# A one-core hybrid attention layer: attention by tiles of rows with the output projection between them, one chunk of 512 columns for two, and a query stack by turns

## The chip, the cores and the metric

The kernel runs on one core of one Trainium2 chip. The metric is device time of one execution in microseconds (us), the median of several runs. The core's engines are PE (matrix products), DVE (vector), ACT (scalar functions and copies), POOL (general purpose) and SP (which issues the transfers). Each runs its own instructions in order, and they wait for each other by semaphores. PEld is PE's loading of stationary operands, which runs beside its products.

## What is computed

The reference is one decoder layer over 512 rows of 1024 features, in float32. A combined projection feeds two groups of eight heads of 64:

```python
h = rms_norm(x, norm_gain)
proj = jnp.einsum('bsd,dc->bsc', h, w_in)          # 3420 columns
# group A: compressed blocks, selected blocks, sliding window; sigmoid gates
o_nsa = g[..., 0:1] * o_cmp + g[..., 1:2] * o_sel + g[..., 2:3] * o_win
o_nsa = o_nsa.reshape(B, S, NSA_WIDTH) * jax.nn.silu(z_n)
# group B: a relu indexer picks 128 keys per query, which are attended
o_dsa = dsa_branch(qd, kd, heads(v_d, Gd), qi_r, ki_r, wi)
o_dsa = o_dsa.reshape(B, S, DSA_WIDTH) * jax.nn.silu(z_d)
mixed = jnp.concatenate([o_nsa, o_dsa], axis=-1)
return x + jnp.einsum('bsc,cd->bsd', mixed, w_out)
```

With 512 rows all eight selected blocks and the whole window are taken, so both are causal attention with different keys and values. The indexer's choice is a mask found by sixteen rounds of "eight largest, strike them out".

## The kernel before, in words

**Precision.** Nearly every product is made of parts: a float32 operand is split in a high part (a cast on ACT, `nc.scalar.copy`) and a low part (a subtraction on DVE or POOL, `split`, L338 and L339), and PE multiplies high by high, high by low and low by high.

**Chunks.** The columns of `w_in` are cut into chunks (`CHUNKS`), each projected for four tiles of 128 rows (`proj`, L372) or transposed (`projT`, L382). `queue_chunk` issues a chunk's loads (256 KB each) and splits; the halves live in a ring of `WBUFS` = 4 slots of 1024 columns, so that a chunk of 256 columns takes two slots and one of 512 columns four. I holds the indexer, C and B the keys and values of group A, Q1 and Q2 its queries (heads of g = 0 and 1), E the keys and values of group B, D its queries, Z0 to Z3 the gates z. `chunk` runs a projection and after each tile its evacuation (norm sums on ACT, rotation on DVE and POOL).

**Attention.** The work is cut into units: `n` i g b is group A, row tile i, head group g, branch b (1 selected, 2 window, 0 compressed), `d` i g 0 is group B. For each (i, g) `qstack` transposes the queries (L577, into one of two S banks of PSUM) and stacks them for the score products: high parts in rows 0 to 63 and again in 64 to 127 (L582, L584, ACT), low parts in a second block (L583, DVE) whose lower rows are zero. `kstack` puts the keys' high parts in rows 0 to 63 (L561) and the low parts in 64 to 127 (L562). The score products (L934, L935) then need two passes. `softmax_of` adds the mask and finds the maximum (L916, DVE), takes exponentials (L918, ACT) and scales (L930, POOL). `transposed` turns the probabilities (L970) and splits them (L971, L972); `times_values` multiplies by the values (L981); `combine` adds the parts (L1008 ACT, L1009 DVE); `mix` multiplies by z and splits the result (L1126 to L1128).

**Output.** `out_half(i, half)` is half of the output projection of row tile i: 24 products over four blocks of `mixed` (L1147), in the two `mm` banks that the projections also use (the last tile's third part in an S bank). Half 0 needs group A's result of that tile, half 1 group B's.

**Order.** `weave` writes the program: it takes attention steps and fills in other work, by credits, until a named unit has ended. Before the change: group A g = 0, tiles 3 to 0, with Q2, E and D as fill; group A g = 1, tiles 3 to 0, with the z chunks and the loads of `wout`; group B, tiles 3 to 0, with `out_half`. Then `set_order` orders all instructions of each engine anew: a list scheduler that runs forward and backward eight times with a cost model, keeps the order with the earliest modelled end and writes it down as dependencies. Its model adds `AGAIN` to ACT instructions that read PSUM, by what went before.

Of the kernel before, what the change touches and what calls it, by code (L numbers as in the profile page):

```python
# [29 lines left out]
    ("E", [(2328, 2584)]),  # L30
# [4 lines left out]
    ("Q2", [(256, 512)]),  # L35
# [27 lines left out]
ARENA = 2824 + 1536 + 256 + 512  # L63
ARENA_R = 5376
# [33 lines left out]
AGAIN = 45, 112, 0  # L98

SPARE = 200  # L100

# [3 lines left out]
def set_order(tc):  # L105
# [40 lines left out]
    def reads_bank(i, e):  # L146

        if e != "Activation":
            return None
        return any("PSUM" in str(getattr(ap.bass_ap.tensor, "space", "")) for w, ap in aps(i) if not w)  # L150
# [62 lines left out]
    bank = [reads_bank(i, e) for i, e in zip(insts, eng)]  # L213
    sums = [len(list(i.outs)) > 1 for i in insts]
# [4 lines left out]
    def turns(due, back=False):  # L219
# [12 lines left out]
        last = [2]  # L232
        there = [0.0] * LANES
        for _ in range(count):
# [4 lines left out]
            k = min((k for k in l if ready[k] <= now), key=lambda k: due[k] + PORT * late * port[k])  # L239
# [11 lines left out]
            if bank[k] is not None:  # L251
                if bank[k]:
                    more = AGAIN[last[0]]
                last[0] = 2 if sums[k] else int(bank[k])
# [37 lines left out]
def tile_hybrid_layer(ctx, tc, xT, x, ng, win, gains, peT, w1, b1, w2, wout, cst, out):  # L292
# [199 lines left out]
    gns = carve([6, 2 * HD], F32)  # L492
    nc.sync.dma_start(gns, gains.rearrange("(o a) b -> o a b", o=1).partition_broadcast(128))
    tabs = carve([2, 2, NT, HD], F32)
    tturn = [0]

    def tables(j, name):
        gn = gns[:, j, None, :]
        c, s = (tabs[:, tturn[0] % 2, x] for x in range(2))
        tturn[0] += 1  # L500
# [51 lines left out]

    def kstack(dst, R, h0, nh, back=False):

        p = ps("T", "kT_ps")
        for t in range(NT):
            c = (NT - 1 - t if back else t) * 128
            nc.tensor.transpose(p[:nh * HD, c:c + 128], R[:, t, h0:h0 + nh, :], ident)
# [5 lines left out]
    qbufs = []  # L564
    for i in range(2):
        qb = carve([2, 4, 128], F32R)
        nc.gpsimd.memset(qb[64:128, 1].bitcast(F32), 0.0)
        qbufs.append(qb)
    qcount = [0]

    def qstack(R, t):
# [16 lines left out]
    ridx = b8.tile([128, NT, 5, HD], F32, tag="ridx", name="ridx")  # L588
    rest = work.tile([128, NT, 28], F32, tag="rest", name="rest", bufs=1)
    for t in (0, 1, 2, 3):  # L590
        p = Ips[t]
        rope(ridx[:, t, 4:5], p[:, :64], 1, cosd[:, t:t + 1, :], sind[:, t:t + 1, :], add=nc.vector)
# [10 lines left out]
    nc.gpsimd.tensor_tensor(ridx[:, :, 4], ridx[:, :, 4], rb.to_broadcast([128, NT, HD]), op=ALU.mult)  # L603
# [10 lines left out]
    kdi = b8.tile([128, 3, S], F32R, tag="kdi", name="kdi")  # L614
# [3 lines left out]
    scores = b8.tile([128, 1152], F32, tag="scores", name="scores")  # L618
    masks = b8.tile([128, 1152], BF16, tag="masks", name="masks")

    def indexer():
        kstack([kdi[:, 2, :]], ridx, 4, 1)
# [3 lines left out]
        for i in (3, 2, 1):  # L626
# [3 lines left out]
            s0 = 64 * i * (i + 1) - 128  # L630
            sc = scores[:, s0:s0 + n]
            for h in range(4):
                p = ps("S", f"idx{i}{h}")
                nc.tensor.matmul(p[:, :n], q[:, 0, h, :], kdi[:, 2, :n], start=True, stop=False)
                nc.tensor.matmul(p[:, :n], q[:, 1, h, :], kdi[:, 2, :n], start=False, stop=True)
# [12 lines left out]
            mbias[i] = masks[:, s0:s0 + n]  # L648
# [14 lines left out]
    kn = [b8.tile([128, 2 * S + 32], F32R, tag=f"kn{g}", name=f"kn{g}") for g in range(2)]  # L663
# [19 lines left out]
    def chunk_C(kv):  # L683
        p = ps("mm", f"C_{kv}")
# [93 lines left out]
    def hidden3():  # L778
        kp = ps("S", "kc_ps")[:64, :64]
        nc.tensor.transpose(kp, FSs["kr"], ident[:64, :64])  # L780
        for g in range(2):
            dst = kn[g][:, K_CMP:K_CMP + 32]
            src_ = kp[:, 32 * g:32 * g + 32]
            nc.scalar.copy(dst[0:64], src_)
            nc.vector.tensor_tensor(dst[64:128], src_, dst[0:64].bitcast(F32), op=ALU.subtract)
        yield 0.1
# [47 lines left out]
    def kb_stack():  # L834
        for b in range(2):
            kstack([k[:, 0:S] if b else k[:, K_SEL:] for k in kn], ST["kb_raw"][b], 0, 2, back=bool(b))
# [4 lines left out]
    def e_first():  # L841
        ST["kd_raw"] = work.tile([128, NT, 2, HD], F32, tag="m2", name="kd_raw", bufs=2)
# [7 lines left out]
    def kd_stack():  # L850
        kstack([kdi[:, 0, :], kdi[:, 1, :]], ST["kd_raw"], 0, 2)
        yield 0.4
# [4 lines left out]
    def queries(name, key, j, gs, nxt, after=()):  # L857

        def first():
# [4 lines left out]
            for g in gs:  # L864
                Rs[key, g] = b8.tile([128, NT, 4, HD], F32, tag=f"R_{key}{g}", name=f"R_{key}{g}")
                ST["ss" + key, g] = sums(f"{key}{g}")

        def evac(p, t):
            for x, g in enumerate(gs):
                heads_of(p[:, 256 * x:256 * x + 256], ST["ss" + key, g], t, Rs[key, g], 4, ST["tab" + key])  # L870

        def done():
            for g in gs:
                norm_of(rs[key, g], ST["ss" + key, g], 4)

# [138 lines left out]
    def units_of(kind, i, g, done):  # L1014
# [20 lines left out]
        if kind == "d":  # L1035
            u.v = [pair(vd[:, j, g]) for j in range(i + 1)]
            u.S = lambda: softmax_steps(kdi[:, g, :max(n, 256)], [(u, slice(0, n), mbias[i])])
# [10 lines left out]
        if i == 0:  # L1048
            us.S = lambda: softmax_steps(k[:, w0:K_SEL + n], [sel(n + 32), win_, cmp(n)])
        else:  # L1050
            uw.S = lambda: softmax_steps(k[:, w0:S], [win_])
            if i < 3:
                us.S = lambda: softmax_steps(k[:, K_CMP:K_SEL + n], [sel(32), cmp(0)])
            else:
                us.S = lambda: softmax_steps(k[:, K_SEL:], [sel(0)])
                uc.S = lambda: compressed_steps(uc, k[:, K_CMP:K_SEL], cmask[:, i, :])
# [33 lines left out]
    def attention(units):  # L1090
# [4 lines left out]
        for k, u in enumerate(units):  # L1095
            ahead.setdefault(max(k - (2 if u.kind == "n" else 1), 0), []).append(u)
# [119 lines left out]
    weave(att, "n010", [  # L1216
# [107 lines left out]
```

## Time and profile before

| what | value |
| --- | --- |
| median of 3 runs | 320.56 us (320.38 to 320.7) |
| the profiled execution | 320.34 us |
| its span, first to last instruction | 318.6 us |
| busy in the span: PE, DVE, ACT, POOL | 312.5, 256.1, 248.1, 243.0 us |
| PE products | 1789 |
| TensorE clock granted | full speed in all 40 slices |

Rows are in us unless marked ns. PE is busy 98% of the span, but the ends of its products are modelled and overlap the next one's start, so short gaps do not show as idle time. Whether PE works or waits is read from the distance of the starts of neighbouring products, against the distance in a stretch without waits.

### The profile page before, as it was taken

How to read it: one execution, taken by the hardware profiler on the slowest of the kernel's cores; microseconds unless marked ns; L12 is line 12 of the kernel's file. 1: busy time of each engine (PE TensorE's matmuls, PEld its weight loads, DVE VectorE, ACT ScalarE, POOL GpSimd, SP SyncE). 2: the span in 40 equal slices, each digit the busy share in tenths (PEclk: the TensorE clock that was granted, in tenths of full speed). 3: DMA queues.
4: the chain of work that ended last, by engine and by line, in shares of the span. 5: the costliest groups of instructions: out<-in, count | busy, mean ns of one | idle time of the engine just before them, and what ended most of it. 6: DMA issues, size and time to landing. Idle time of an engine off the chain costs nothing.

```text
span 318.6 us, 6139 instructions
## 1 busy us (share of the span) xinstructions
PE 312.5 (98%) x1789; PEld 267.7 (84%) x1789; DVE 256.1 (80%) x773; ACT 248.1 (78%) x813; POOL 243.0 (76%) x418
## 2 busy tenths in 40 slices
PE   8999999999999999999999999999999999999995
PEld 5997888999989998888887888788877778888885
DVE  4978532999999999999999999999997887825301
ACT  6962855999889999899998988889988999943200
POOL 3179897988998999886699999995859987873200
PEclk9999999999999999999999999999999999999999
DMA  7990553445230133000031053021220533403011
GB/s 256 417 352 33 139 160 115 150 116 181 70 99 2 37 99 100 2 1 0 3 87 47 2 165 88 16 82 48 69 66 2 163 102 100 149 19 102 31 66 66
DMA packets 14945, 30.28 MB, mean 95 GB/s; under 512 B 1792, under 2 KB 2176, under 8 KB 14912
## 3 DMA queue, kind: packets, MB, share of 16 engines
q1 hardware_dynamic: 14912, 29.90, 30.0%
q8 instruction: 14, 0.23, 0.3%
q14 instruction: 19, 0.16, 0.2%
HBM read 27.79 MB, written 2.10 MB: 94 GB/s over the span
## 4 chain that ended last, share of the span: by engine, by line
PE 62%; DVE 21%; ACT 9%; issue 3%; DMA 2%; POOL 1%; SPq 1%; DVEq 0%; POOLq 0%
PE out L1147 13%; PE D L372 7%; PE B L372 7%; PE on L981 5%; PE T_n L970 4%; PE E L372 4%; PE z L382 4%; DVE scores L647 3%; DVE m L646 3%; PE od L981 3%; DMA xw<-in_xT_dram 2%; DVE P_d L916 2%; PE s_n L934 2%; DVE ptl L972 2%; PE s_n L935 2%
## 5 line engine op out<-in xcount | busy, mean ns | idle before, releaser
L918 ACT ACTIVATE P_n<-P_n,arena 128x512 f32<-128x512 f32 (+3 forms) x64 | 35.9, 563 | 4.2 <-DVE arena L916 3.7
L930 POOL TENSOR_SCALAR P_n<-P_n,arena 128x512 f32<-128x512 f32 (+3 forms) x64 | 33.2, 538 | 1.5
L916 DVE CUSTOM_DVE_ANT_0 P_n<-s_n,arena 128x512 f32<-128x512 f32 (+3 forms) x64 | 34.0, 542 | 0.3
L972 DVE TENSOR_TENSOR ptl<-T_n,pth 128x512 fp32r<-128x512 f32 x40 | 27.2, 683 | 0.6 <-ACT pth L971 0.2
L382 PE MATMUL z<-hThi,whi_Z 128*128 128x512 f32 x64 | 27.0, 422 | 0.1
L646 DVE MAX8 m<-scores 128x8 f32<-128x512 f32 (+2 forms) x48 | 26.4, 550 | 0.2
L647 DVE MATCH_REPLACE8 scores<-m,scores 128x512 f32<-128x512 f32 (+2 forms) x48 | 26.0, 541 | 0.1
L382 PE MATMUL z<-hThi,wlo_Z 128*128 128x512 f32 x64 | 25.4, 396 | 0.0
L382 PE MATMUL z<-hTlo,whi_Z 128*128 128x512 f32 x64 | 25.2, 393 | 0.0
L970 PE MATMUL T_n<-arena,P_n 128*128 128x128 f32 x160 | 24.6, 272 | 0.0
L1147 PE MATMUL out<-wohi,mx 128*128 128x512 f32 (+1 forms) x72 | 23.5, 377 | 0.0
L971 ACT CAST pth<-T_n 128x512 fp32r<-128x512 f32 x40 | 23.1, 581 | 0.4
L970 PEld LDWEIGHTS T_n<-arena,P_n 128*128 128x128 f32 x160 | 19.9, 140 | 3.7
L1147 PE MATMUL out<-whi_wo,mx 128*128 128x512 f32 (+1 forms) x72 | 22.2, 374 | 0.0
L339 POOL TENSOR_TENSOR wlo_Z<-raw_Z,whi_Z 128x512 fp32r<-128x512 f32 x16 | 20.6, 1303 | 1.6 <-ACT whi_Z L338 1.6
L339 POOL TENSOR_TENSOR w1l<-raw_w,w1h 128x512 fp32r<-128x512 f32 x16 | 20.5, 1294 | 1.5 <-ACT w1h L338 1.4
L972 DVE TENSOR_TENSOR ptl<-T_d,pth 128x512 fp32r<-128x512 f32 x20 | 13.8, 689 | 8.5 <-ACT pth L971 8.3
L930 POOL TENSOR_SCALAR P_d<-P_d,arena 128x512 f32<-128x512 f32 (+3 forms) x32 | 16.7, 543 | 4.2 <-DVE arena L920 4.1
L934 PE MATMUL s_n<-kn,arena_r 128*128 128x512 f32 (+4 forms) x56 | 19.8, 353 | 0.1
L981 PE MATMUL on<-pth,arena_r 128*128 128x512 f32 x48 | 19.8, 413 | 0.0
L918 ACT ACTIVATE P_d<-P_d,arena 128x512 f32<-128x512 f32 (+3 forms) x32 | 17.8, 559 | 1.9 <-DVE arena L916 1.8
L981 PE MATMUL on<-ptl,arena_r 128*128 128x512 f32 x48 | 18.9, 395 | 0.0
(277 smaller groups left out, 1193.2 us busy)
## 6 DMA issues: line engine op xcount, KB each, us to landing
raw_w<-in_w_dram SPq DMA_DIRECT2D x16, 256.0 KB, 3.0
raw_Z<-in_win_dram SPq DMA_DIRECT2D x16, 256.0 KB, 2.7
wor<-in_wout_dram SPq DMA_DIRECT2D x16, 256.0 KB, 2.8
raw_Q<-in_win_dram SPq DMA_DIRECT2D x8, 256.0 KB, 2.8
raw_D<-in_win_dram SPq DMA_DIRECT2D x8, 256.0 KB, 2.7
xres<-in_x_dram SPq DMA_DIRECT2D x8, 256.0 KB, 2.8
out_dram<-xres SPq DMA_DIRECT2D x7, 256.0 KB, 2.0
xw<-in_xT_dram SPq DMA_DIRECT2D x2, 860.0 KB, 8.7
```

Of the source, the lines that this page charges most:

```text
L339: engine.tensor_tensor(lo, raw, hi.bitcast(F32), op=ALU.subtract)
L372: nc.tensor.matmul(out_ps, a[:, k, tsl], b, start=(k == 0 and b is hi and a is hT["hi"]), stop=(k == KB - 1 and a is hT["lo"]))
L382: nc.tensor.matmul(out_ps, b[:, csl], a[:, k, :], start=(k == 0 and b is hi and a is hT["hi"]), stop=(k == KB - 1 and b is lo))
L646: nc.vector.max(m8, sc)
L647: nc.vector.match_replace(sc, m8, sc, -3e38)
L916: nc.vector.tensor_tensor_reduce(P[:, h], src_, mask, u.r[:, h:h + 1], 3e38, op0=ALU.add, op1=ALU.min, accum_out=m[:, h:h + 1])
L918: nc.scalar.activation(P[:, h], P[:, h], AF.Exp, bias=m[:, h:h + 1], scale=-1.0, accum_out=l[:, h:h + 1])
L930: nc.gpsimd.tensor_scalar(P[:, hh], P[:, hh], l[:, hh:hh + 1], 1.0 if u.gate is not None else 0.5, op0=ALU.mult, op1=ALU.mult)
L970: nc.tensor.transpose(p[:, h * 128:(h + 1) * 128], u.P[:, h, j * 128:(j + 1) * 128], ident)
L972: nc.vector.tensor_tensor(pl, p, ph.bitcast(F32), op=ALU.subtract)
L981: nc.tensor.matmul(o, u.v[j], pp, start=(u.first and j == 0 and x == 0), stop=(end and x == 1))
L1147: nc.tensor.matmul(p, a, b[:, csl], start=(k == 0 and b is hi and a is mx[0]), stop=(k == 7 and a is mx[1]))
```

## The change

Five things are changed.

- **One chunk for two.** E is gone from `CHUNKS`; its 256 columns follow those of Q2, and `queries` gets hooks for E's own start, evacuation and end.
- **Query and key stacks.** `qstack` writes the high parts of an odd head into rows 64 to 127 and its low parts into rows 0 to 63, those of an even head the other way round; each query is stacked once, high and low in one column, and multiplied by a key block with high parts in both halves and one with low parts in both halves. `kstack` fills both halves of both blocks by a new helper, `key_parts`. The indexer's key is written twice by POOL, so that its transpose has it in both halves.
- **Order of the attention and the output.** After group A g = 0, each tile does its group A g = 1 units and then its two group B units; the halves of the output projection of a tile stand between the units of the next.
- **The scheduler's model.** `AGAIN` is replaced by `TURN`: 125 ns on ACT and 118 ns on DVE, less idle time, where an instruction starts on other rows than the one before it, and a leaning of a quarter of that to instructions on the same rows. Due times are also carried back along the dependencies.
- **Places.** Chunk C's products stand in O banks and not in mm banks; tables, gains, scores and masks are tiles of their own and not parts of one large tile; the query stack's look-ahead is one unit instead of two where the unit before is of group B.

```diff
 CHUNKS = [
     ("I", [(2840, 2908), (1280, 1304), (2584, 2840)]),
-    ("E", [(2328, 2584)]),
     ("D", [(1816, 2328)]),
...
-    ("Q2", [(256, 512)]),
+    ("Q2", [(256, 512), (2328, 2584)]),
...
-AGAIN = 45, 112, 0
+TURN = {"Activation": 125, "DVE": 118}
+
+CHOICE = 0.25
...
+    def rows_of(i, e):
+
+        if e not in TURN:
+            return None
+        first = []
+        for w, ap in sorted(aps(i), key=lambda x: x[0]):
+            row = list(ap.ap)[0][0]
+            if free(ap) > 1:
+                first.append(ap.bass_ap.offset // row if row else 0)
+        return tuple(first) if any(first) else ()
...
+        if not back:
+            due = [d - h for d, h in zip(due, hurry)]
+            for k in reversed(range(count)):
+                for j in before[k]:
+                    due[j] = min(due[j], due[k] - costs[j][0])
...
-            k = min((k for k in l if ready[k] <= now), key=lambda k: due[k] + PORT * late * port[k])
+            k = min((k for k in l if ready[k] <= now), key=lambda k: due[k] + PORT * late * port[k]
+                    + (CHOICE * TURN[e] if e in TURN and rows[k] != last[e] else 0))
...
-                    more = AGAIN[last[0]]
-                last[0] = 2 if sums[k] else int(bank[k])
+            if e in TURN:
+                if rows[k] != last[e]:
+                    more = max(TURN[e] - (start[k] - idle[e]), 0)
+                last[e] = rows[k]
...
+    def key_parts(dst, src_, o):
+
+        hi, lo = dst
+        at, to = slice(64 * o, 64 * o + 64), slice(64 - 64 * o, 128 - 64 * o)
+        nc.scalar.copy(hi[at], src_)
+        nc.vector.tensor_tensor(lo[at], src_, hi[at].bitcast(F32), op=ALU.subtract)
+        nc.scalar.copy(hi[to], src_)
+        nc.scalar.copy(lo[to], lo[at].bitcast(F32))
+
...
         for g in range(nh):
-            src_ = p[g * HD:(g + 1) * HD, :]
-            nc.scalar.copy(dst[g][0:64], src_)
-            nc.vector.tensor_tensor(dst[g][64:128], src_, dst[g][0:64].bitcast(F32), op=ALU.subtract)
...
+            key_parts(dst[g], p[g * HD:(g + 1) * HD, :], g)
...
-        qv = q.rearrange("p s (a b) q -> p s a b q", b=2)
+        qv = q.rearrange("p (a b) q -> p a b q", b=2)
         for o in range(2):
-            src_ = pv[o * 64:(o + 1) * 64]
-            nc.scalar.copy(qv[0:64, 0, :, o, :], src_)
-            nc.vector.tensor_tensor(qv[0:64, 1, :, o, :], src_, qv[0:64, 0, :, o, :].bitcast(F32), op=ALU.subtract)
-            nc.scalar.copy(qv[64:128, 0, :, o, :], src_)
+            hi, lo = slice(o * 64, o * 64 + 64), slice(64 - o * 64, 128 - o * 64)
+            nc.scalar.copy(qv[hi, :, o, :], pv[hi])
+            nc.vector.tensor_tensor(qv[lo, :, o, :], pv[hi], qv[hi, :, o, :].bitcast(F32), op=ALU.subtract)
         return q
...
-        p = ps("mm", f"C_{kv}")
+        p = ps("O", f"C_{kv}")
...
     def scores_of(p, q, h, k):
-        nc.tensor.matmul(p, q[:, 0, h, :], k, start=True, stop=False)
-        nc.tensor.matmul(p, q[:, 1, h, :], k, start=False, stop=True)
+        for x in range(2):
+            nc.tensor.matmul(p, q[:, h, :], k[:, x], start=(x == 0), stop=(x == 1))
...
     units = []
-    for g in range(2):
-        for i in (3, 2, 1, 0):
-            units += units_of("n", i, g, nothing)
     for i in (3, 2, 1, 0):
+        units += units_of("n", i, 0, nothing)
+    for i in (3, 2, 1, 0):
+        units += units_of("n", i, 1, nothing)
         for g in range(2):
-            units += units_of("d", i, g, lambda i=i, g=g: mix(1, i, g))
+            units += units_of("d", i, g, nothing if i == 3 else lambda i=i, g=g: mix(1, i, g))
     att = attention(units)
     weave(att, "n000", [
-        queries("Q2", "q", 0, [1], "E", {0: hidden3(), 1: hidden1(1), 3: hidden2(1)}),
-        call(queue_chunk, "D"),
-        chunk("E", e_evac, lambda: norm_scale([ST["kd_raw"]], ST["ss_kd"]), e_first),
+        queries("Q2", "q", 0, [1], "D", {0: hidden3(), 1: hidden1(1), 3: hidden2(1)},
+                (e_first, lambda p, t: e_evac(p[:, 256:], t), lambda: norm_scale([ST["kd_raw"]], ST["ss_kd"]))),
         queries("D", "d", 3, [0, 1], "Z0"),
         kd_stack(),
     ], RA, X1, LEAD)
-    weave(att, "n010", [
+    weave(att, "d310", [
         zchunk(0, "Z1"),
...
-    for g in range(2):
-        mix(0, 3, g)
-    weave(att, "d310", [out_half(3, 0)], 0.0, X3)
+    for half in range(2):
+        for g in range(2):
+            mix(half, 3, g)
     for i in (2, 1, 0):
+        weave(att, f"n{i}10", [out_half(i + 1, 0)], RA, X3)
         for g in range(2):
             mix(0, i, g)
-        weave(att, f"d{i}10", [out_half(i + 1, 1), out_half(i, 0)], RA, X4)
-    weave((), None, [out_half(0, 1)], 1.0)
+        weave(att, f"d{i}10", [out_half(i + 1, 1)], RA, X4)
+    weave((), None, [out_half(0, 0), out_half(0, 1)], 1.0)
     set_order(tc)
```

## Rows read from the trace of the kernel before

**Rows 1.** Windows by stage: stretch, its length, busy us and count of each engine, clock.

```profile
90.00:168.00 78.00, 77.84 (x484) 68.35 (x483) 76.31 (x259) 72.17 (x280) 66.41 (x124) 1.00 0.16 45
168.00:248.00 80.00, 79.28 (x410) 65.40 (x408) 76.21 (x247) 70.00 (x212) 69.77 (x121) 1.00 0.21 60
248.00:318.60 70.60, 66.87 (x363) 55.83 (x361) 36.33 (x95) 38.32 (x107) 37.63 (x54) 1.00 0.27 86
```

**Rows 2.** Pieces of the chain that ended last: start, length, engine, tile, count.

```profile
33.20 21.76 PE B L372 x96
...
99.90 3.83 PE E L372 x32
...
120.16 0.69 PE D L372 x3
...
299.32 16.03 PE out L1147 x93
```

**Rows 3.** Waits for line 584 (us in total, times, longest), and PE's timeline at one.

```profile
PEld s_n L934 <- ACT arena_r L584: 0.7, 2, 0.4
...
PEld s_d L934 <- ACT arena_r L584: 0.5, 1, 0.5
...
236.46 0.40 PE L382 MATMUL z<-hThi,wlo_Z 128*128 128x512 f32 x1
236.94 0.45 PE L934 MATMUL s_d<-kdi,arena_r 128*128 128x384 f32 x1
```

**Rows 4.** PE's timeline, three transposes of queries and the product before each.

```profile
238.73 0.34 PE L935 MATMUL s_d<-kdi,arena_r 128*128 128x384 f32 x1
239.55 0.44 PE L577 MATMUL qT_ps<-arena,R_d 128*128 128x128 f32 x2 [0.48 <-DVE arena L916]
...
256.10 0.39 PE L934 MATMUL s_d<-kdi,arena_r 128*128 128x256 f32 x1
256.50 0.44 PE L577 MATMUL qT_ps<-arena,R_d 128*128 128x128 f32 x2
...
264.47 0.38 PE L970 MATMUL T_d<-arena,P_d 128*128 128x128 f32 x2
265.03 0.44 PE L577 MATMUL qT_ps<-arena,R_d 128*128 128x128 f32 x2 [0.17 <-DVE arena L916]
```

**Rows 5.** ACT's groups by line and shape: count, busy us, mean ns, idle before.

```profile
L584 ACT CAST arena_r<-qT_ps 64x256 fp32r<-64x256 f32 x38 | 13.9, 367 | 4.6 <-DVE arena_r L583 3.7
...
L561 ACT CAST kn<-kT_ps 64x512 fp32r<-64x512 f32 x4 | 2.3, 580 | 0.0
```

**Rows 6.** ACT's timeline, copies on the same rows and on other rows.

```profile
233.26 0.36 ACT L582 CAST arena_r<-qT_ps 64x256 fp32r<-64x256 f32 x1
233.51 0.37 ACT L1008 COPY on<-on 64x256 f32<-64x256 f32 x1
...
234.49 0.37 ACT L582 CAST arena_r<-qT_ps 64x256 fp32r<-64x256 f32 x1
234.89 0.37 ACT L1008 COPY on<-on 64x256 f32<-64x256 f32 x1
```

**Rows 7.** DVE's timeline, two on all rows, and two on different halves.

```profile
86.53 0.41 DVE L512 TENSOR_TENSOR rt<-Q,arena 128x256 f32<-128x256 f32 x1
86.87 0.41 DVE L517 TENSOR_TENSOR rt<-Q,arena 128x256 f32<-128x256 f32 x1
...
299.45 0.88 DVE L1009 TENSOR_TENSOR od_d<-od,od_d 64x256 f32<-64x256 f32 x2 [0.43 <-ACT od_d L1008]
```

**Rows 8.** DVE's evacuation of chunk C: count, ns, first and last start.

```profile
L695 DVE TENSOR_TENSOR kt<-C,arena x8: 415/433/443, 29.2 to 35.2; 64x256 f32<-64x256 f32 x8
```

**Rows 9.** POOL's timeline, splits of D's weights while E is projected.

```profile
107.68 3.81 POOL L339 TENSOR_TENSOR wlo_D<-raw_D,whi_D 128x512 fp32r<-128x512 f32 x3
```

**Rows 10.** The timeline at the end: last product with values, last split of mix.

```profile
298.92 0.40 PE L981 MATMUL od<-ptl,arena_r 128*128 128x512 f32 x1
...
303.19 0.74 POOL L1128 TENSOR_TENSOR mx<-od_d,mx 128x256 fp32r<-128x256 f32 x1 [0.52 <-ACT mx L1127]
```

More of the change, by code (lines that the diff above doesn't have):

```diff
@@ L212, in set_order @@
     port = [shared(i, e) for i, e in zip(insts, eng)]
-    bank = [reads_bank(i, e) for i, e in zip(insts, eng)]
-    sums = [len(list(i.outs)) > 1 for i in insts]
+    rows = [rows_of(i, e) for i, e in zip(insts, eng)]
+    hurry = [max((h for _, ap in aps(i)[-1:] for x, h in HURRY.items() if ap.bass_ap.tensor.name.startswith(x)), default=0)
+             for i in insts]
     def gap(j, k):
@@ L231, in turns @@
         start = [0.0] * count
-        last = [2]
+        last = {e: () for e in TURN}
+        if not back:
[3 more added lines that the diff above has]
+                    due[j] = min(due[j], due[k] - costs[j][0])
         there = [0.0] * LANES
@@ L490, in tile_hybrid_layer @@
     csin = cs[:64, C_CSIN:C_CSIN + HD]
-    gns = carve([6, 2 * HD], F32)
+    gns = b8.tile([128, 6, 2 * HD], F32, tag="gns", name="gns")
     nc.sync.dma_start(gns, gains.rearrange("(o a) b -> o a b", o=1).partition_broadcast(128))
-    tabs = carve([2, 2, NT, HD], F32)
-    tturn = [0]
     def tables(j, name):
         gn = gns[:, j, None, :]
-        c, s = (tabs[:, tturn[0] % 2, x] for x in range(2))
-        tturn[0] += 1
+        c, s = (work.tile([128, NT, HD], F32, tag="tab" + x, name="tab" + x, bufs=3) for x in "cs")
         nc.gpsimd.tensor_tensor(c, cosd, gn[:, :, :HD].to_broadcast([128, NT, HD]), op=ALU.mult)
@@ L557, in kstack @@
             c = (NT - 1 - t if back else t) * 128
-            nc.tensor.transpose(p[:nh * HD, c:c + 128], R[:, t, h0:h0 + nh, :], ident)
-        for g in range(nh):
-            src_ = p[g * HD:(g + 1) * HD, :]
-            nc.scalar.copy(dst[g][0:64], src_)
-            nc.vector.tensor_tensor(dst[g][64:128], src_, dst[g][0:64].bitcast(F32), op=ALU.subtract)
[L564 to L568, printed above, removed]
+            if nh == 1:
+                nc.tensor.transpose(p[:, c:c + 128], R[:, t, h0:h0 + 2, :], ident)
+            else:
+                nc.tensor.transpose(p[:, c:c + 128], R[:, t, h0:h0 + nh, :], ident)
+        if nh == 1:
+            hi, lo = dst[0]
+            nc.scalar.copy(hi, p)
+            nc.vector.tensor_tensor(lo, p, hi.bitcast(F32), op=ALU.subtract)
+            return
+        for g in range(nh):
+            key_parts(dst[g], p[g * HD:(g + 1) * HD, :], g)
+    qbufs = [carve([4, 128], F32R) for _ in range(2)]
     qcount = [0]
@@ L612, in tile_hybrid_layer, with two @@
     nc.gpsimd.tensor_scalar(gate, gate, 0.25, 0.25, op0=ALU.mult, op1=ALU.add)
[L614 removed]
+    def two(v, cols=slice(None)):
+        return v[:, 0, cols], v[:, 1, cols]
+    kix = b8.tile([128, 2, S], F32R, tag="kix", name="kix")
     mbias = {0: tri[:, S - 128:S]}
[L618 to L619 removed]
     def indexer():
[L622 removed]
+        kstack([two(kix)], ridx, 4, 1)
         yield 0.4
@@ L661, in tile_hybrid_layer @@
     vcs = vall[:, NT * 4:]
-    kn = [b8.tile([128, 2 * S + 32], F32R, tag=f"kn{g}", name=f"kn{g}") for g in range(2)]
+    kn = [b8.tile([128, 2, 2 * S + 32], F32R, tag=f"kn{g}", name=f"kn{g}") for g in range(2)]
     K_CMP, K_SEL = S, S + 32
@@ L781, in hidden3 @@
         for g in range(2):
[L782 to L785, printed above, removed]
+            key_parts(two(kn[g], slice(K_CMP, K_CMP + 32)), kp[:, 32 * g:32 * g + 32], 0)
         yield 0.1
@@ L835, in kb_stack @@
         for b in range(2):
-            kstack([k[:, 0:S] if b else k[:, K_SEL:] for k in kn], ST["kb_raw"][b], 0, 2, back=bool(b))
+            kstack([two(k, slice(0, S) if b else slice(K_SEL, None)) for k in kn], ST["kb_raw"][b], 0, 2, back=bool(b))
             yield 0.4
@@ L850, in kd_stack @@
     def kd_stack():
-        kstack([kdi[:, 0, :], kdi[:, 1, :]], ST["kd_raw"], 0, 2)
+        kstack([two(ST["kdi"][:, g]) for g in range(2)], ST["kd_raw"], 0, 2)
         yield 0.4
@@ L855, in tile_hybrid_layer, with queries @@
     rs = {(key, g): carve([NT, 4], F32) for key in "qd" for g in range(2)}
-    def queries(name, key, j, gs, nxt, after=()):
+    def queries(name, key, j, gs, nxt, after=(), rest=(None, None, None)):
         def first():
@@ L866, in first @@
                 ST["ss" + key, g] = sums(f"{key}{g}")
+            if rest[0]:
+                rest[0]()
         def evac(p, t):
@@ L874, in done @@
                 norm_of(rs[key, g], ST["ss" + key, g], 4)
+            if rest[2]:
+                rest[2]()
         return chunk(name, evac, done, first, after)
@@ L1095, in attention @@
         for k, u in enumerate(units):
-            ahead.setdefault(max(k - (2 if u.kind == "n" else 1), 0), []).append(u)
+            lead = 2 if u.kind == "n" and (k == 0 or units[k - 1].kind == "n") else 1
+            ahead.setdefault(max(k - lead, 0), []).append(u)
         for k in range(-AHEAD, len(units) + 1):
```

41 lines of the change are left out of this document (20 added, 21 removed).

## The prediction, made before the change was run

> **What bounds the kernel now.** I read the windows by stage first, then the chain of waits for the pace of products, then PE's timeline for its gaps. In the windows [rows 1] PE is busy 77.84 of 78 us, then 79.28 of 80. DVE stands beside it with 76.3 and 76.2, ACT with 72 and 70. So from 90 to 248 us two engines are full, and the first question is which one sets the end. The third window answers it: from 248 us on DVE and ACT work 36 and 38 of 70.6 us, while PE still has 66.87. What DVE does before 248 us could end later without harm; what PE does could not. The chain of waits says the same at its end: one unbroken piece of 93 output products, 16.03 us, up to 315.35 us [rows 2]. The last 3.25 us of the span are the last add and its store.
>
> A busy PE proves little here, since modelled ends cover short gaps. The pace does: B runs 96 products of 512 columns in 21.76 us, 227 ns each, D three in 0.69, 230 ns each, and E 32 products of 256 columns in 3.83, 120 ns each [rows 2]. Where starts stand further apart than that, PE waited. The large gaps are few and of two kinds. Score products wait for line 584, the second copy of a query stack: three waits, 1.2 us together on the weight load's side; at 236.46 the next product starts 0.48 us later instead of 0.23 [rows 3]. And transposes of queries wait until DVE's L916 has freed an S bank: 0.82, 0.40 and 0.56 us between starts [rows 4]. A product of 384 columns is worth 0.17 us at the pace of rows 2, one of 256 columns 0.12, two transposes some 0.22 (an estimate: the second follows within the row's 0.44 us, whose end is modelled). The three therefore lose 0.65, 0.28 and 0.34 us, 1.27 together. So the kernel has little to give: PE's own work, and gaps of a few us.
>
> **One chunk for two.** Q2 and E are 192 products of 256 columns (8 blocks, 3 parts, 4 tiles, each) at 120 ns: 23.0 us. The new chunk is 96 of 512 columns: 22.1 us at D's pace, 21.8 at B's. PE gains 0.9 us (0.9 to 1.2), all of it on the path. I take D's pace, since this chunk too runs beside attention. The loads are 8 of 256 KB on SP either way, with the same 8 casts on ACT and 8 subtractions on POOL; the evacuations are the same instructions.
>
> **Where that chunk's weights stand.** It fills all four slots; before, Q2 and E took two each, and POOL could split three of D's eight pieces at 107.68 us [rows 9], while E was still projected and 12 us ahead of D's first product at 120.16 [rows 2]. Now D's first piece can be written only when the last tile of the new chunk has used its slot. A split costs POOL 1.27 us [rows 9]: eight are 10.2 us, against 24 products or 5.5 us in that last tile. The shortfall is 4.7 us if PE had nothing else to do, nothing if attention fills it. From 90 to 168 us E and D take 96 products each, 33.6 us, and the rest of Q2 a few more of the 78; more than half of PE's work there is attention, so I take 0 and keep 4.7 as the far end. Queued behind such a wait on PE is everything in the written order of PE, attention's products too.
>
> **Stacks.** Each of 19 query stacks loses two copies on ACT: line 584 goes, 38 copies or 13.9 us [rows 5]. Six stacks of keys get two copies more each: 12 at 0.58 us, 7.0 us [rows 5]; two short ones for the compressed keys add under 1 us. ACT thus loses about 6 us of work, and a score product waits for the DVE subtraction and no copy after it. Turns matter too: two copies on the same rows start 0.25 us apart, on other rows 0.40 [rows 6]; the old stack changes rows at nearly each of four copies, the new at one of two. I take 0.7 us off PE's path of the 1.2 [rows 3] (0 to 1.2), since some of those scores will then wait for line 583. The keys' longer way (0.6 us for a further copy) stands before the first scores, where Q2 is cover; without the cover it costs 0 to 1.2. The products themselves keep number and columns: two passes before and after. The indexer's key costs POOL one multiplication of double length and no wait on PE.
>
> On DVE the price goes the other way: two subtractions between halves take 0.88 us back to back, 0.44 apart, while two on all rows start 0.34 apart [rows 7]. A low part that is written to the other half costs some 0.10 us twice per stack, 3.8 us over 19 stacks, spread over 200 us. The Trainium skill speaks against the change here (VectorE: DVE Perf Modes, section Two Vector instructions with no wait between them): a Vector instruction that starts in another quadrant than the last one on that memory is held until the earlier ones have finished. By that rule the new stack is held at both of its subtractions, the old at about one, and the trace agrees in kind with the 0.10 us above. For the sum: of the 19 stacks about five fall between 90 and 168 us, where DVE has 1.7 us left [rows 1]; they cost 1.0, which fits. I take 0 (0 to 1.0).
>
> **Order of attention and output.** Before, group B's units and 45 us of output products stood together at the end, and z with 12 units of group A. The three transposes of rows 4 are at that seam, where z runs out and output products cannot start until a tile is done. Now z (192 products of 0.23 us, 44 us) stands beside five large units, and the output beside fifteen. Is there enough for DVE and ACT in the end? PE had 66.87 us after 248 us [rows 1]. Twelve units of group A and z's 44 us made up most of its 79.28 us before that; the nine smaller of the twelve, half of the 35 us that z leaves, come on top: some 84 us. DVE had 36.3 us there, and the nine bring less than half of the 76.2 us of the window before, which also holds z and the indexer's rounds: under 74 in all; ACT likewise 38.3 and under 35. 74 of 84 leaves PE the bound. I take 1.1 of the 1.27 us away (0 to 1.27), and give 0.1 to new places of the same kind. What is late next is PE itself.
>
> **Chunk C in O banks.** The second product of C now waits until DVE has read the first, that is for the first four of eight evacuations, which begin at 29.2 us [rows 8] and end near 31.0. PE had begun it some 3.5 us earlier. B's first four blocks are there as cover, 12 products or 2.7 us. I take 0.2 us (0 to 0.9).
>
> **The scheduler's model** touches no instruction. It now prices the turns of rows 6 and 7, which the old one did not; whether its order is better cannot be read here. I take 0, and bound it by the gaps that it could open or close, about 1 us each way.
>
> **The sum**, against the profiled execution of 320.34 us: 0.9 + 0.7 + 1.1 off, 0.1 + 0.2 on, that is 2.4 off: 317.9. The median of the runs is 0.2 above the profiled one: 318.1.
>
> **Rivals.** First, **all gaps close**: 1.2 for the chunk, 1.2 and 1.27 for the two kinds of wait, and 1 us of small gaps through the better model: 4.7 off, 315.9. For it speaks that DVE and ACT get slack before 248 us; against it that every list order leaves some gaps. Second, **gaps move**: chunk 0.9 and nothing else off, 0.3 on for turns and banks: 319.9, no change that can be measured. For it: two S banks serve the same 16 query stacks, and fifteen units in the last part ask for them with more to do on DVE. It is also the case that the order does not arrive, since the scheduler sorts the engines anew. Third, on the other side, **D's weights come late**: PE waits for POOL's splits for the 4.7 us above; 318.1 + 4.7 = 322.8. It decides where POOL, busy 66.4 of 78 us [rows 1], cannot do the eight splits in the time of the last tile and of the attention beside it: for it speaks that three were made 12 us ahead before, against it that D's products can be spaced by attention. Fourth, **an open end**: from the last product with values to the last split of mix are 5.0 us [rows 10], covered before by 16 us of output products [rows 2]. Attention ends later now; if only one half of tile 0 were left, 5.7 us, a late start could cost up to 5.0: 323.1.
>
> **How the numbers follow.** Forecast 318.1: 0.45, its own range 317.0 to 319.5. All gaps close, 315.9: 0.17. Gaps move, 319.9 to 321: 0.14. D's weights late, 322.8: 0.17. Open end, 323.1: 0.07. The range goes from 315.4 (the second case and half of the scheduler's bound) to 321.9 (half of the late weights); about 0.16 lies above it and 0.03 below. A measurement of this kernel tells apart about 0.2%, 0.64 us: faster is below 319.9 (0.62), the same up to 321.2 (0.14), slower above (0.24).
>
> **What would show it.** Q's and E's rows become 96 products about 0.23 us apart; line 584's successor is gone, and no score waits for ACT's second copy; at the seam from z to output the starts on PE keep the pace; DVE and ACT are busy until near the end, not only to 280 us. Wrong is the forecast if PE's timeline shows waits for D's low parts around 115 to 130 us, or a hole before the last tile's second half, or new waits of transposes for L916.

## The result, and the profile after

The changed kernel takes 318.2 us (317.49 to 318.69), the kernel before beside it 320.47: a ratio of 0.9926, 95% interval 0.9911 to 0.9941. Forecast were 318.1. The profiled execution is the fastest of the four, 317.49 us with a span of 315.7, so what is read from it lies some 0.7 us on the good side.

Busy us, share and count of each engine over the span, from the page of the changed kernel:

```profile
PE 310.4 (98%) x1693; PEld 261.6 (83%) x1693; DVE 260.1 (82%) x773; ACT 243.7 (77%) x791; POOL 242.3 (77%) x416
```

The windows by stage of the changed kernel, with the columns of [rows 1]:

```profile
90.00:168.00 78.00, 77.53 (x411) 64.28 (x409) 75.68 (x245) 72.83 (x294) 66.52 (x142) 1.00 0.16 45
168.00:248.00 80.00, 80.00 (x413) 66.79 (x413) 76.24 (x226) 61.83 (x156) 64.41 (x92) 1.00 0.27 76
248.00:315.70 67.70, 64.50 (x367) 54.68 (x365) 43.61 (x138) 41.82 (x139) 40.06 (x72) 1.00 0.20 63
```

PE is full, the more so from 168 to 248 us (80.00, was 79.28); DVE and ACT have more to do after 248 us than before (43.61 and 41.82 us, were 36.33 and 38.32). All that PE's own queue still waited for (us in total, times, longest):

```profile
PE I L441 <- DVE arena L443: 1.4, 1, 1.4
PE s_n L964 <- DVE arena_r L608: 0.5, 1, 0.5
PE kT_ps L584 <- ACT kb_raw L557: 0.3, 1, 0.3
```

The first is the start of the kernel and stood in the kernel before as well. The waits of [rows 3] and [rows 4] are gone; the other two lie at 92 and 73 us, not at the seam. The one at 92 us is a score that waits for the low part of a new query stack (L608).

Pieces of the chain that ended last:

```profile
35.03 19.59 PE B L388 x84
...
216.94 17.25 PE z L398 x74
...
296.35 16.17 PE out L1178 x93
```

Here is what the forecast did not have. B runs at 233 ns per product (19.59 / 84), and ran at 227 in [rows 2]; the instructions are the same and nothing is waited for. z runs at 233, too. Taken from the starts of all products of 512 columns that follow each other without a wait, the mean is 230.6 ns before (713 of them) and 232.7 after (793). So the right total hides two things: PE's waits shrank by more than forecast, and its products became slower.

A split of the two spans, worked out from the starts of PE's products (each shape at its median distance in the kernel before, 231 ns for 512 columns): PE's own work 304.4 to 303.6 us, what the products of 512 columns run over or under that -0.3 to +1.4, all other gaps 9.5 to 5.9. That is 0.9 and 3.6 off and 1.6 on, 2.9 in all, as the spans say. The forecast had 1.5 us for the gaps (0.7 and 1.1 off, 0.1 and 0.2 on) and nothing for the pace.

### The profile page after: what moved, and what is told of

It is laid out like the page before. It is cut to its first block, busy times and chain, and to the rows that moved or that the text cites. A ratio compares the mean times of both kernels' runs of the same rounds, so it can differ in the third digit from the quotient of the medians.

```text
span 315.7 us, 5949 instructions
## 1 busy us (share of the span) xinstructions
PE 310.4 (98%) x1693; PEld 261.6 (83%) x1693; DVE 260.1 (82%) x773; ACT 243.7 (77%) x791; POOL 242.3 (77%) x416
## 4 chain that ended last, share of the span: by engine, by line
PE 90%; ACT 2%; POOL 2%; issue 2%; DMA 1%; DVE 1%; DVEq 0%; POOLq 0%; ACTq 0%
PE z L398 14%; PE out L1178 14%; PE on L1010 7%; PE B L388 7%; PE D L388 7%; PE s_n L964 6%; PE T_n L999 6%; PE Q L388 5%; PE I L477 5%; PE C L398 4%; PE s_d L964 3%; PE od L1010 3%; PE T_d L999 3%; PE qT_ps L602 1%; PE I L441 1%
## 5 line engine op out<-in xcount | busy, mean ns | idle before, releaser
L964 PE MATMUL s_n<-kn,arena_r 128*128 128x512 f32 (+4 forms) x112 | 29.8, 348 | 0.5 <-DVE arena_r L608 0.5
L398 PE MATMUL z<-hThi,whi_Z 128*128 128x512 f32 x64 | 26.1, 411 | 0.0
L1178 PE MATMUL out<-whi_wo,mx 128*128 128x512 f32 (+1 forms) x72 | 24.6, 381 | 0.0
L964 PEld LDWEIGHTS s_n<-kn,arena_r 128*128 128x128 f32 x112 | 20.0, 188 | 4.7 <-DVE arena_r L608 0.9
L388 PE MATMUL Q<-whi_Q,hThi 128*128 128x256 f32 (+1 forms) x64 | 22.1, 345 | 0.0
L388 PE MATMUL Q<-wlo_Q,hThi 128*128 128x256 f32 (+1 forms) x64 | 22.0, 347 | 0.0
L388 PE MATMUL Q<-whi_Q,hTlo 128*128 128x256 f32 (+1 forms) x64 | 21.7, 341 | 0.0
```

The lines of the kernel that those rows point to most:

```text
L388: nc.tensor.matmul(out_ps, a[:, k, tsl], b, start=(k == 0 and b is hi and a is hT["hi"]), stop=(k == KB - 1 and a is hT["lo"]))
L398: nc.tensor.matmul(out_ps, b[:, csl], a[:, k, :], start=(k == 0 and b is hi and a is hT["hi"]), stop=(k == KB - 1 and b is lo))
L964: nc.tensor.matmul(p, q[:, h, :], k[:, x], start=(x == 0), stop=(x == 1))
L1178: nc.tensor.matmul(p, a, b[:, csl], start=(k == 0 and b is hi and a is mx[0]), stop=(k == 7 and a is mx[1]))
```

## The experiments

Each time is compared with runs of the kernel before on the same chip (medians 320.17 to 320.74); the ratios are the safer numbers. "Place" below is the address of a buffer in a partition of SBUF (the memory that the engines work from), modulo 512 bytes, in the compiled program; "one place" means that the transposed hidden states and the weight slots have the same.

| run | median us | ratio (95%) | against before, us |
| --- | --- | --- | --- |
| changed kernel | 318.2 | 0.9926 (0.9911 to 0.9941) | -2.4 |
| e1, changed, weights moved | 315.84 | 0.9851 (0.9838 to 0.9863) | -4.8 |
| e2, before, weights moved apart | 321.44 | 1.0026 (1.0015 to 1.0038) | +0.8 |
| e3, order alone | 322.21 | 1.0056 (1.0034 to 1.0077) | +1.8 |
| e5, order alone, one place | 321.08 | 1.0010 (0.9997 to 1.0022) | +0.3 |
| e4, changed, old order | 319.35 | 0.9964 (0.9952 to 0.9976) | -1.2 |
| e11, e4 at one place | 318.17 | 0.9933 (0.9920 to 0.9945) | -2.1 |
| e6, chunk alone | 320.16 | 0.9982 (0.9971 to 0.9993) | -0.6 |
| e9, stacks alone | 321.75 | 1.0049 (1.0037 to 1.0061) | +1.6 |
| e10, stacks and chunk | 322.24 | 1.0059 (1.0047 to 1.0071) | +1.9 |
| e8, e1 with old stacks | 315.96 | 0.9844 (0.9823 to 0.9865) | -5.0 |
| e7, e1 with less room | 318.48 | 0.9927 (0.9905 to 0.9949) | -2.3 |
| e12, e7 with the old model | 319.48 | 0.9980 (0.9969 to 0.9990) | -0.6 |

### Why the products are slower: e1, e2, e5

In the kernel before, the transposed hidden states (`hThi`, `hTlo`) and all weight slots stand at place 160. In the changed kernel the smaller arenas (the large tiles that small ones are cut from) put the hidden states at 128, the slots stayed at 160. In the compiled programs the largest tiles that stay all along (the two arenas and the two of hidden states) stand largest first. The float32 arena has 20512 bytes in the kernel before, 40 times 512 and 32 more, and stands ahead of the hidden states of 16384 bytes each; in the changed kernel it has 13344, 26 times 512 and 32 more, and stands behind them, so its odd 32 bytes shift the slots alone. The theory: a product is slower when its two operands stand at different places. e1 is the changed kernel with an arena 32 bytes shorter, which puts both at 128; every engine's order is the same.

```diff
-ARENA = 2824 + 1536 + 256 + 512 - 768 - 1024
+ARENA = 2824 + 1536 + 256 + 512 - 768 - 1024 - 8
```

> The changed kernel with one large tile cut by 32 bytes, so that the weight slots stand 32 bytes lower in memory: at the same place within 64 bytes as hT, as they stood to each other before the change. Every instruction and every engine's order is the changed kernel's. Theory of addresses: the changed kernel's products of 512 columns run 2 ns slower (232.7 ns against 230.6 in the median stretches, B 234 against 227) because weights and hT no longer stand alike; here B returns to 227 ns and some 790 products give back 1.6 us, 316.6 us where the changed kernel has 318.2. Rival, the pace belongs to the execution and not to the addresses: B stays at 234 ns in some executions and the time is 318.2.

Measured 315.84. The same pieces of e1's chain:

```profile
35.24 19.22 PE B L388 x84
...
216.33 16.81 PE z L398 x74
```

z falls from 233 to 227 ns per product, with the same 74 products in the same order; B's median step from 234 to 227. The mean of all products of 512 columns is 229.9 ns: 2.3 us less over 793, which is the gain. e1 also beats both kernels.

e2 turns it round: the kernel before, with the arena 32 bytes shorter and `hTlo` 32 bytes longer, so that `hTlo` comes to 128 while `hThi` and the slots stay at 160. Every engine's order is that of the kernel before.

```diff
-ARENA = 2824 + 1536 + 256 + 512
+ARENA = 2824 + 1536 + 256 + 512 - 8
...
-        hT[part] = const.tile([128, KB, S], F32R, tag="hT" + part, name="hT" + part)
+        more = 8 * (part == "lo")
+        hT[part] = const.tile([128, KB * S + more], F32R, tag="hT" + part, name="hT" + part)
+        hT[part] = hT[part][:, :KB * S].rearrange("p (k c) -> p k c", k=KB)
```

> The kernel before with hTlo 32 bytes lower, so that the low parts of h no longer stand like the weight slots within 64 bytes; hThi and the weights keep their relation, and no instruction changes. Theory of addresses: the third of the projections' products that reads hTlo runs 7 ns slower in B, the others as before; with 208 such products of 512 columns (B, C, D, z) up to 1.4 us and at least 0.4: 320.9 to 321.9. Rival, the pace belongs to the execution: 320.5, B at 227 ns throughout or at 234 throughout.

```profile
34.47 22.18 PE B L374 x96
```

B now needs 231 ns (227 in [rows 2]), and by step: 226.8 from `whi` by `hThi` to `wlo` by `hThi`, both at 160; 234.8 from there to `whi` by `hTlo`; 231.5 back from `hTlo` to `hThi` (32 steps each, from the starts). Only the steps that touch the buffer that was moved are slow.

e5 belongs to e3, the order alone, whose slots lay at 288 and hidden states at 160. Two tiles of keys were declared longer, the order is e3's on every engine, and the slots come to 160.

```diff
-    kn = [b8.tile([128, 2 * S + 32], F32R, tag=f"kn{g}", name=f"kn{g}") for g in range(2)]
+    kn = [b8.tile([128, 2 * S + 128], F32R, tag=f"kn{g}", name=f"kn{g}")[:, :2 * S + 32] for g in range(2)]
```

> The kernel before with the new order alone, as in the run of the order alone, and with identical order on every engine; only the two tiles of keys are declared 384 bytes longer each (the added columns are never used), which moves the weight slots from 128 bytes beside the transposed hidden states (addresses modulo 512) to the same place. Theory A (the 512-column products are slower when their two operands lie at different places modulo 512): the products of chunk B fall from 232 to 227 ns, the mean of all 713 by about 1.3 ns, so 0.9 us: 321.3 us, still slower than the kernel before by its added gaps of 0.9. Rival B (the new order itself, by its traffic on the ports of SBUF, slowed the products, and the address counts only within 64 or 128 bytes): products of chunk B stay at 232 ns, 322.2 us. Rival C (the order is worth a gain by itself once the addresses are alike): under 320.3 us.

PE's timeline inside B, first e3, six products apart, then the piece of e5's chain:

```profile
41.71 0.39 PE L372 MATMUL B<-wlo_B,hThi 128*128 128x512 f32 x1
...
43.11 0.39 PE L372 MATMUL B<-wlo_B,hThi 128*128 128x512 f32 x1
```

```profile
33.31 21.77 PE B L372 x96
```

1.40 us for six is 233 ns; 21.77 / 96 is 227. So 128 bytes apart is slow as well (232 by the median of all), and nothing but places in memory was changed. All kernels fit (e2, with one of its operands moved, as shown): with one place for both, 160 or 128, B's median step is 227 (the kernel before, e1, e5 and all runs below but e4), 32 bytes apart 234 (the changed kernel and e4), 128 apart 232 (e3).

### The order: e3, e4, e11

e3 is the kernel before with the new order of the units, the new weaves and the shorter look-ahead. e4 is the changed kernel with the old ones.

```diff
-    for g in range(2):
-        for i in (3, 2, 1, 0):
-            units += units_of("n", i, g, nothing)
     for i in (3, 2, 1, 0):
+        units += units_of("n", i, 0, nothing)
+    for i in (3, 2, 1, 0):
+        units += units_of("n", i, 1, nothing)
...
```

> The kernel before with the new order of attention and output alone (units, weaves and the query stack's look-ahead); chunks, stacks and the scheduler's model are as before. Theory of the prediction: the seam's waits go, 1.1 us: 319.4. Rival, the scheduler's model closes the gaps: no change, 320.5. Rival, the new order without the new stacks brings more waits of transposes for S banks: 321.5 or more.

> The changed kernel with the old order of attention and output; chunk, stacks and model are the new ones. Theory of the prediction: the order was worth 1.1 us, so 319.3. Rival, the stacks and the model close the seam's gaps as well and the order is worth nothing: 318.2. Where both this and the order alone show 1 us or more, the parts add; where only one does, they stand in for each other.

Alone, the order does not gain: 1.8 us slower, of which the place accounts for some 1.5 (e5 by the ratios: +0.3, not told apart from none). The waits of [rows 4] are nearly gone in e5, others came (PE's longest but for the start of the kernel):

```profile
PE qT_ps L577 <- POOL P_n L930: 0.4, 1, 0.4
PE kT_ps L558 <- ACT kb_raw L544: 0.3, 1, 0.3
PE on L981 <- ACT pth L971: 0.2, 1, 0.2
PE on L981 <- POOL ptl L967: 0.2, 1, 0.2
PE T_n L970 <- DVE arena L916: 0.2, 1, 0.2
```

Within the changed kernel it is worth 1.2 us (0.9964 against 0.9926), and 2.6 with the operands at one place (e11 against e1).

> The changed kernel with the old order of the attention, as in an earlier run (319.35), identical order on every engine, and the shifted arena (weights and hidden states at one place modulo 512). Address theory: 2.4 us less, as with the new order: 317.0 us; the order is then worth 1.2 us, and what lies between this and the run of chunk and stacks together is the scheduler's model. Rival (the two effects are one: slower products only filled time that was waited anyway): above 318 us.

e11 has e4's order, with hidden states and weights placed as in e1 (the transposed probabilities stand at 0; in e1 they stand at 128). It gained 1.0 us by the ratios and not 2.4, and its 318.17 us are the rival's case: its mean step fell from 232.5 to 230.5 ns, and its other gaps grew by 0.7 us, by the split used above.

z's median step is 227 in e1 and 231 in e11, though both operands stand at 128; in the kernel before, which has e11's order of z and attention, it is 231 too. The starts show where this comes from. Steps from one z product to the next that have z products on both sides, too, take 227 ns in e1 and in the kernel before (medians of 84 and 16), 229.5 in e11 (16). Steps with another product beside them take 231 in e1 (54), 232 in the kernel before and in e11 (90 and 91). The old order breaks z up by attention, so few of its steps are of the first kind. Why a step beside another product is longer was not tried.

### The chunk and the stacks: e6, e9, e10, e8

e6 is the kernel before with the merged chunk alone; the places are those of before.

```diff
-    ("E", [(2328, 2584)]),
...
-    ("Q2", [(256, 512)]),
+    ("Q2", [(256, 512), (2328, 2584)]),
...
```

> The kernel before with the merged chunk alone (second queries and DSA keys and values as one chunk of 512 columns); its weight slots and hidden states lie at the same addresses as before. Theory (the step of the prediction): 96 products of 256 columns in pairs become 96 fewer, 0.9 us less TensorE work with nothing else late: 319.4 to 319.8 us. Rival: ACT and DVE are the limit of that stretch, the time saved is waited for elsewhere: 320.4 to 320.8 us. Second rival: the longer evictions hold the bank of the next tile: over 321 us.

320.16, between the theory and its first rival: 0.6 us less (0.2 to 0.9). By the median two thirds of PE's 0.9 us of work arrive; the interval does not exclude the whole.

e9 is the kernel before with the new `qstack`, `kstack`, `key_parts` and the two arrays of keys, e10 adds e6's chunk.

```diff
-            nc.scalar.copy(qv[0:64, 0, :, o, :], src_)
-            nc.vector.tensor_tensor(qv[0:64, 1, :, o, :], src_, qv[0:64, 0, :, o, :].bitcast(F32), op=ALU.subtract)
-            nc.scalar.copy(qv[64:128, 0, :, o, :], src_)
+            nc.scalar.copy(qv[hi, :, o, :], pv[hi])
+            nc.vector.tensor_tensor(qv[lo, :, o, :], pv[hi], qv[hi, :, o, :].bitcast(F32), op=ALU.subtract)
...
```

> The kernel before with the new query and key stacks alone (two copies by ACT for a query stack in place of four, keys in two arrays); weight slots and hidden states at the same addresses as before. By the prediction's term (0.7 of 0 to 1.2 us): 319.9 us. Rival, from the run of the changed kernel with the old stacks, which was as fast as with the new ones: the removed copies were hidden, 320.5 to 320.8 us. At the upper bound of the term: 319.4 us.

> The kernel before with the merged chunk and the new stacks, the old order of the attention and the scheduler's old model; same addresses as before. The merged chunk alone gave 320.16 against 320.74. If the parts add up, the chunk 0.6 and the stacks 0 to 0.7: 319.4 to 320.1 us. If the merged chunk gives its whole 0.9 once ACT has fewer copies to do: 319.0 to 319.3 us.

Neither expectation held: the stacks alone cost 1.6 us. In e9 no score waits for a second copy any more. Scores now wait on PEld for DVE's L929 (L916 of the kernel before) and L906, and the output for its parts. The waits for L929 sum to 2.6 us, and in the kernel before those for L916 to 2.5, but there most of them were of transposes (the first row below, then three of e9):

```profile
PEld qT_ps L577 <- DVE arena L916: 1.7, 4, 0.8
```

```profile
PEld s_n L948 <- DVE arena L929: 1.5, 4, 0.6
...
PEld s_d L948 <- DVE z L906: 0.7, 1, 0.7
...
PEld out L1160 <- POOL mx L1141: 0.6, 1, 0.6
```

DVE's subtraction waits for ACT's first copy 4.0 us in all in e9, 1.6 in the kernel before, 0.9 in the changed one (three rows, in this order):

```profile
DVE arena_r L595 <- ACT arena_r L594: 4.0, 6, 1.8
```

```profile
DVE arena_r L583 <- ACT arena_r L582: 1.6, 4, 0.7
```

```profile
DVE arena_r L608 <- ACT arena_r L607: 0.9, 3, 0.4
```

Taking the copy away did not take the time away: with it gone, what came next in DVE's and ACT's order held the scores. No one wait makes up the 1.6 us: by the split used above all gaps grow from 9.5 to 11.1 us, in many short pieces, and the scheduler ordered every engine anew. e10 shows what one instruction's position in such an order can cost:

```profile
PE C L381 <- ACT rest L603: 2.1, 1, 2.1
```

Chunk C's first product waits for a bank that ACT has yet to read, and the edit changes neither instruction: 2.1 us at 20 us, as much as e10's whole loss.

e8 undoes the stacks in the changed kernel at one place (the memory they take leaves three raw weight buffers for four); e7 is the control, e1 with three raw buffers, two pairs of tables for three and one tile of masks for three.

> The changed kernel with the shifted addresses, and the query and key stacks made as in the kernel before (a third copy by ACT for each half of a query stack, keys in one copy), three raw weight buffers for the memory that this takes. Against 315.84 for the shifted addresses alone, and the control with less room run beside it. By the prediction's term for the stacks (0.7 of 0 to 1.2): 316.5 us. If the stacks carry all of the gaps that the order does not explain (3.6 less 1.8 in the traces): 317.6 us. If the removed copies were hidden: 315.8 to 316.0 us.

> A control: the changed kernel with the shifted arena (weights and hidden states at one place modulo 512), and less memory: three raw weight buffers in place of four, two pairs of tables in place of three, the masks in one tile. If none of these buffers is waited for: 315.7 to 316.2 us, as with the shifted arena alone (315.84). If the loads of weights need the fourth buffer: over 316.5 us.

e8 is as fast as e1, 0.9844 against 0.9851, the case of hidden copies: no gain of the stacks is to be seen there either. What the missing raw buffer did to e8 stays open. If it cost anything, the old stacks are the faster ones here. The control failed to price it, for it took away more than e8 does and lost 2.4 us against e1 by the ratios. Part of that is the clock. PE's timeline, and PE's busy time and granted clock in three stretches of it:

```profile
95.96 0.70 PE L965 MATMUL s_n<-kn,arena_r 128*128 128x512 f32 x2 [0.54 <-DVE arena_r L608]
97.40 0.72 PE L388 MATMUL Q<-whi_Q,hThi 128*128 128x512 f32 x1 [0.74 <-DVE arena_r L824]
97.92 0.63 PE L388 MATMUL Q<-wlo_Q,hThi 128*128 128x512 f32 x1
98.35 0.63 PE L388 MATMUL Q<-whi_Q,hTlo 128*128 128x512 f32 x1
```

```profile
95.00:96.00 1.00, 0.46 (x3) 1.00 0.00 0
96.00:97.30 1.30, 0.66 (x2) 1.00 0.00 0
97.30:100.80 3.50, 3.40 (x8) 0.52 0.00 0
```

After the two waits, of 0.54 and 0.74 us, the granted clock was 0.52 of full speed over 3.5 us, nearly all of it at the lower level of 1.2 GHz, and products came 0.43 us apart in place of 0.23: some 1.6 us on top of the waits, by the starts. Only this run was profiled; two others of e7's six have the same mean granted clock, 0.995 (the three took 319.0 to 319.4 us). The other three, at 1.000, took 317.3 to 318.0, still 1.4 to 2.1 us above e1, and what cost that is not known.

### The scheduler's model: e12

e12 is e7 with the old model.

```diff
-TURN = {"Activation": 125, "DVE": 118}
+AGAIN = 45, 112, 0
...
-                for j in before[k]:
-                    due[j] = min(due[j], due[k] - costs[j][0])
...
```

> The control with less room (318.48) with the scheduler's old cost model in place of the turns; all else alike, addresses too. If the model is worth what is left over between the parts (chunk and stacks together some 319.7, against 317.0 for all but the order): 2.7 us slower, 321.2 us. By the prediction, which gave it 0 of -1 to +1: 317.5 to 319.5 us.

The old model is 1.7 us slower by the ratios (0.9980 against 0.9927), although e7 carries the lower clock in half its runs. The 319.48 us alone would still lie in what the prediction allowed; but e7 and e12 ran on different chips, and the kernel before is 0.57 us faster on e12's. PE's longest waits in e12 are of the kind that a list order makes: two for a bank that DVE's L931 frees, and one before the hidden layer of the compressed keys.

```profile
PE s_n L950 <- DVE arena L931: 1.3, 2, 1.0
PE hid L743 <- DVE scr L737: 0.6, 1, 0.6
```

The same step is seen from e10 to e11 (1.0059 to 0.9933, 4.0 us): new are the model, the tiles of their own for tables, gains, scores and masks, and C's banks, with the order of the units still old. 2.1 of the 4.0 are e10's one wait. Whether the turns' price or the carried due times do it was not tried, nor whether another order of the same list would have done as well by chance.

## Why the prediction was right in total, and where its steps failed

- **What bounds.** Right. PE is busy 80.00 of 80 us in the stage where it had been 79.28 [rows 1].
- **One chunk**, 0.9. PE's products fell from 1789 to 1693 and its own work by 0.9 us, as forecast. Alone it gave 0.6 (0.2 to 0.9).
- **D's weights late**, taken as 0. Right. POOL splits as the slots come free, the first at 112.3, the last at 125.4 us, and D's first product comes 0.23 us after the one before it. Attention spaces D's products, as the prediction supposed: the 96 are spread from 120.3 to 158.5 us.

```profile
L355 POOL TENSOR_TENSOR wlo_D<-raw_D,whi_D x8: 1283/1293/1299, 112.3 to 125.4; 128x512 fp32r<-128x512 f32 x8
```

```profile
119.06 0.39 PE L388 MATMUL Q<-whi_Q,hTlo 128*128 128x512 f32 x1
...
120.08 0.40 PE L1010 MATMUL on<-pth,arena_r 128*128 128x512 f32 x1
120.31 0.40 PE L388 MATMUL D<-whi_D,hThi 128*128 128x512 f32 x1
```

- **Stacks**, 0.7. This step failed. A wait put down to the second copy [rows 3] was taken as time that goes with the copy. Alone the stacks cost 1.6 us, in the changed kernel they gave nothing that was seen (e8). The prediction did expect some scores to wait for the subtraction instead; one does, for 0.5 us.
- **DVE's turns**, 0 of 0 to 1.0, from a price of 3.8 us. The price was read from another instruction (the two of L1009 in [rows 7] are additions of `combine`), but the starts of the stacks' own subtractions bear it out. Each takes as long as before (422 ns, was 418). Of those that followed another DVE instruction without a wait, in the kernel before 16 began 0.03 us after its end and 15 some 0.08 us ahead of it; in the changed kernel all 32 began after. Of the instructions behind a subtraction 8 of 31 began after its end, now 32 of 35. These are 40 more starts that lose some 0.11 us each, 4.4 us. None of it is seen in the time (e8 against e1), so the 0 stands as far as is known. That DVE's busy time grew by a like 4.0 us is luck: stacks alone bring 1.6, the order alone, with old stacks, 4.8. Busy us and count of each engine in e9 and in e5:

```profile
PE 314.0 (98%) x1789; PEld 267.7 (84%) x1789; DVE 257.7 (81%) x773; ACT 244.6 (76%) x791; POOL 242.2 (76%) x416
```

```profile
PE 313.0 (98%) x1789; PEld 268.1 (84%) x1789; DVE 260.9 (82%) x773; ACT 250.9 (79%) x813; POOL 243.8 (76%) x418
```

- **Order**, 1.1. Its size holds within the changed kernel (1.2; 2.6 with the operands at one place), and alone its sign does not. The waits at the seam are gone, as said; that others take their place, which the prediction gave to a rival ("gaps move") for the whole, is what happens to this part by itself.
- **Chunk C in O banks**, 0.2. It cost nothing: nine of B's products stand ahead of C's second projection, which follows at 0.23 us.

```profile
28.13 0.40 PE L388 MATMUL B<-whi_B,hTlo 128*128 128x512 f32 x1
28.36 0.40 PE L398 MATMUL C<-hThi,whi_C 128*128 128x512 f32 x1
```

- **The open end** did not come: the last product with values starts at 295.95 us, the 93 output products from 296.35 on cover the 5 us behind it.
- **The scheduler's model**, 0 of -1 to 1. Of the terms in the sum the most wrong in size: 1.7 us or more (e12), with the other parts as they are. The prediction costed each part by itself. Under the old model the stacks cost time alone, the order gains none, and all parts together, with less room, gain 0.6 (e12); that the new model is what makes them gain more is argued from e12 and not shown part by part.
- **Not in the sum at all**: the places of the operands. The smaller arena moved the hidden states by 32 bytes against the weights, and this cost 2.4 us (e1). The prediction has no term for it. That the total came out to 0.1 us is luck: two misses of about 2 us cancel.

## What to carry to other kernels

A wait that the profile puts down to one instruction is not yet time that goes when that instruction goes: where a scheduler orders the engines anew, the parts of a change do not add up, so cost them together, in the order that they will run in. After any edit of buffers, compare the pace of products that the edit did not touch: if their starts have moved apart with no wait between, look at where the operands stand before looking at the schedule.

## What the hardware showed that was not expected

- B's products of 512 columns in float32 follow each other 227 ns apart where the weights and the hidden states stand at one place modulo 512 bytes, 234 with 32 bytes and 232 with 128 bytes between them. Other distances were not tried, nor the reason. z's products, at one place, keep 227 in a run of their own (84 steps in e1) and take 231 to 232 beside other products.
- After two waits of PE, of 0.54 and 0.74 us, the granted clock lay at its lower level for most of 3.5 us (0.52 of full speed) in the profiled run of e7; two more of its six runs have the same mean clock.
